# Mamba-2 scan layer: cumulative sums one convolution tile sooner, the first group's decay on VectorE behind its x tiles, its exponentials behind the last silu

## The chip, the core and the metric

The kernel runs on one core of a Trainium2 chip (trn2). The metric is the device time of one execution in microseconds (us). The engines of the core are named as the profile names them: PE is TensorE (matmuls; PEld its weight loads), DVE is VectorE, ACT is ScalarE, POOL is GpSimd, and SP only starts DMA transfers here.

## The reference, cut to what matters

Two macaron layers: each is half a SwiGLU, a mixer, half a SwiGLU, with a layer norm behind each. Layer 0 mixes with sparse attention, layer 1 with a Mamba-2 scan. The change lies in that scan, over 256 tokens in two chunks of 128, with 32 heads in 4 groups of 8:

```python
z, xbc, dt = split(x @ w_in)            # gate 2048, x/B/C 2048+512+512, dt 32
xbc = silu(conv_b + sum_k xbc_pad[:, k:k+seq] * conv_w[k])   # 4 taps
xs, b_in, c_in = split(xbc)
dt = softplus(dt + dt_bias); a_dt = dt * -exp(a_log)
a_cs = cumsum(a_dt, over the chunk)
decay = exp(where(tri, a_cs[l] - a_cs[s], -inf))             # per head, 128 x 128
y_diag = ((c @ b.T) * decay) @ (xs * dt)
states = b.T @ (xs * dt * exp(a_cs[-1] - a_cs)); prev = scan over chunks
y = y_diag + (c @ prev) * exp(a_cs) + xs * d_skip
out = rms_norm(y * silu(z), per group) * norm_g @ w_out
```

## The kernel before

All weights stream from DRAM in units of 128 x 1024 (`raw`), issued by SP. ACT casts each to a high part (`wh`, line 188), DVE subtracts to get the low part (`wl`, line 207), and PE multiplies in three passes (high by high, high by low, low by high; lines 380 to 382). Ten units fit in the ring of high and low parts. `W.pump(n)` makes the low parts that are due and then n more high parts; `W.lows()` makes only the low parts that are due and starts loads.

The order of the work is written out by hand: each engine has its instructions in the order in which the code issues them.

In `ssd` the names are these. `z_half(g, t, i, u)` is half of the gate projection of group g for chunk t, 12 matmuls, with a silu on ACT (line 1116) behind its second half. `bc_tile(i)` (8 of them) and `xs_tile(g, i, u)` (4 for each group) are convolution tiles: 24 matmuls into a PSUM bank `pxs`, one of three that take turns; then `conv`: an identity with bias on ACT (line 1135), three multiply-adds on DVE (line 1138) and a silu on ACT (line 1130). That silu is put in a list and issued only behind the identity of the next tile, or by `flush()`.

`cumsums()` multiplies `adt` by triangles on PE, takes two small exponentials on ACT (`dend`, `eacs`), copies on DVE, and has POOL store the sums to DRAM (`scr`). `decay_load(t, g)` has POOL load them back, spread over all partitions, into `M[t, g]` (128 x 1024, 8 heads). `decay_seg` subtracts the sums, head by head, 8 instructions: on ACT as a relu with the sign turned (line 1183) where `on_act` is set, else on DVE (line 1185). `decay_exp` is one exponential on ACT (line 1188), `decay_cb` a product with `cbm` (c by b, under the triangle) on DVE (line 1192).

`x_tok(t, g)` transposes the four x tiles of a group on PE (line 1207) and scales them on DVE (lines 1209, 1210). `diag(t, g)` multiplies `M[t, g]` by them (PE, line 1220), `state` and `carry` take care of the step from chunk 0 to chunk 1, `gate` adds and multiplies by the silu of z (DVE, lines 1237, 1238), `square`, `root` and `norm` scale, and `y_tr` transposes back.

Group 0's decay is made ahead of the loop over groups, between its own four x tiles, and with relus on ACT. Groups 1 to 3 make theirs inside the loop, on DVE, one group ahead. The last half of z of group 1 (`z_half(1, 1, 1, uz)`) is kept for the end of this stretch.

Of the kernel before, what the change touches and what calls it, by code (L numbers as in the profile page):

```python
# [258 lines left out]
def trunk_kernel(ctx: ExitStack, tc: tile.TileContext, widths, x, ln_g, ln_b, wts, kvg, convp,  # L259
# [12 lines left out]
    def nm(s):  # L272
        cnt[0] += 1
        return f"{s}_{cnt[0]}"
# [4 lines left out]
    def f2(s):  # L279
        return wk.tile([128, 512], F32, name=nm(s), tag="f2", bufs=9)  # L280
# [13 lines left out]
    def pmm():  # L294
        return psum.tile([128, 512], F32, name=nm("pmm"), tag="pmm", bufs=2)
# [11 lines left out]
    def ptr():  # L307
        return psum.tile([128, 512], F32, name=nm("ptr"), tag="ptr", bufs=2)

    W = Weights(nc, f4, ring, wts, widths, SLOTS, RAWS)  # L310
# [705 lines left out]
    def ssd(xT, u, ln_i):  # L1016
# [39 lines left out]
        def cumsums():  # L1056
            pt = ptr()
            for t in range(2):
                v = adt[:, t * 32:(t + 1) * 32]
                nc.tensor.matmul(pt[:, t * 32:(t + 1) * 32], tri, v, start=True, stop=True)  # L1060
                nc.tensor.matmul(pt[:32, 128 + t * 128:256 + t * 128], v, tri, start=True, stop=True)
            nc.tensor.matmul(pt[:, 64:96], after, adt[:, :32], start=True, stop=True)
            nc.scalar.activation(dend, pt[:, 64:96], AF.Exp)
            nc.scalar.activation(eacs, pt[:, 32:64], AF.Exp)
            at = f1("at")
            nc.vector.tensor_copy(at[:32], pt[:32, 128:384])
            nc.gpsimd.dma_start(scr.rearrange("t h l -> h t l"), at[:32].rearrange("p (t l) -> p t l", t=2))
            for t in range(2):
                acs[t] = tiny("acs")
                nc.vector.tensor_copy(acs[t], pt[:, t * 32:(t + 1) * 32])  # L1070
# [49 lines left out]
        def decay_load(t, g):  # L1120
            M[t, g] = f4("M")
            nc.gpsimd.dma_start(M[t, g], scr[t:t + 1, g * 8:(g + 1) * 8, :].rearrange("o h l -> o (h l)")
                                .to_broadcast([128, 1024]))
# [4 lines left out]
        def flush():  # L1128
            while late:
                nc.scalar.activation(*late.pop(0), AF.Silu)  # L1130
# [11 lines left out]
        def bc_tile(i):  # L1142
            ps = xbank()
            proj_b(ps[:, :256], xT, u + 10 + i, False)
            W.free(u + 10 + i)
            dst = bT if i < 4 else cTt
            conv(ps, 16 + i, dst[:, (i % 4) * 256:(i % 4 + 1) * 256])
            W.pump(1 + i % 2)
# [4 lines left out]
        def b_tr():  # L1153
            pt = pspare(4)
            for g in range(SG):
                nc.tensor.transpose(pt[:, g * 128:(g + 1) * 128], bT[:, g * 256:g * 256 + 128], ident)
            nc.scalar.copy(btok, pt)

        def cb(t):
            pt = pspare(4)  # L1160
            for g in range(SG):
                c = slice(g * 256 + t * 128, g * 256 + (t + 1) * 128)
                nc.tensor.matmul(pt[:, g * 128:(g + 1) * 128], bT[:, c], cTt[:, c], start=True, stop=True)
            nc.vector.tensor_mul(cbm[:, t * 512:(t + 1) * 512].rearrange("p (g l) -> p g l", g=SG),
                                 pt.rearrange("p (g l) -> p g l", g=SG),
                                 tri[:, None, :].to_broadcast([128, SG, 128]))
# [3 lines left out]
        def hv(ap):  # L1170
            return ap.rearrange("p (h d) -> p h d", h=8)

        def hb(ap, g):
            return ap[:, g * 8:(g + 1) * 8][:, :, None].to_broadcast([128, 8, 64])

        def decay_seg(t, g, on_act=False):

            m = M[t, g]
            for h in range(8):
                hs = slice(h * 128, (h + 1) * 128)  # L1180
                a = acs[t][:, g * 8 + h:g * 8 + h + 1]
                if on_act:
                    nc.scalar.activation(m[:, hs], m[:, hs], AF.Relu, bias=a, scale=-1.0)
                else:
                    nc.vector.tensor_scalar(m[:, hs], m[:, hs], a, 0.0, op0=ALU.subtract, op1=ALU.min)

        def decay_exp(t, g, on_act=False):
            nc.scalar.activation(M[t, g], M[t, g], AF.Exp, scale=-1.0 if on_act else 1.0)

        def decay_cb(t, g):  # L1190
            mv = M[t, g].rearrange("p (h l) -> p h l", h=8)
            nc.vector.tensor_mul(mv, mv, cbm[:, None, t * 512 + g * 128:t * 512 + (g + 1) * 128]
                                 .to_broadcast([128, 8, 128]))
# [4 lines left out]
        def x_tok(t, g):  # L1198

            if t:  # L1200
                pt = ptr()
            elif g < 3:
                pt = psum.tile([128, 512], F32, name=nm("pxt"), tag="acc11", bufs=1)
            else:
                pt = pmm()
            for i in range(4):
                nc.tensor.transpose(pt[:, i * 128:(i + 1) * 128], xsT[g][i][:, t * 128:(t + 1) * 128], ident)
            y[t], xd[t] = f2("xdt"), f2("xtok")
            nc.vector.tensor_mul(hv(y[t]), hv(pt), hb(dt[:, t * 32:(t + 1) * 32], g))
            nc.vector.tensor_mul(hv(xd[t]), hv(pt), hb(dsk, g))  # L1210

        def x_end(g):
            xe[g] = f2("xe")
            nc.vector.tensor_mul(hv(xe[g]), hv(y[0]), hb(dend, g))
# [43 lines left out]
        def xs_tile(g, i, uu):  # L1258
            if not i:
                xsT[g] = []  # L1260
            ps = xbank() if g < 3 else pmm()
            proj_b(ps[:, :256], xT, uu, False)
            W.free(uu)
            o = wk.tile([128, 256], F32, name=nm("xsT"), tag="xsT", bufs=5)
            conv(ps, g * 4 + i, o)
            xsT[g].append(o)
            W.pump(1)
# [29 lines left out]
        uz = u + 6  # L1297
        for i in range(8):
            bc_tile(i)
            if i == 6:  # L1300
                cumsums()
                for t in range(2):
                    decay_load(t, 0)
        u += 18
        for i in range(4):
            xs_tile(0, i, u + i)
            if i == 0:
                b_tr()
                cb(0)
                cb(1)  # L1310
                decay_seg(0, 0, True)
            elif i == 1:
                decay_seg(1, 0, True)
            elif i == 2:
                decay_exp(0, 0, True)
                decay_exp(1, 0, True)
            else:
                decay_cb(0, 0)
        z_half(1, 1, 1, uz)
        flush()  # L1320
        W.pump(2)
        decay_cb(1, 0)
        u += 4
        py = {}
        for g in range(SG):
            if g < 2:
                f = [lambda i=i: xs_tile(g + 1, i, u + i) for i in range(4)]
                f += [lambda t=t, i=i: (z_half(g + 2, t, i, u + 4), W.pump(1)) for t in range(2) for i in range(2)]
            elif g == 2:
                x3 = [lambda i=i: xs_tile(3, i, u + 2 * i) for i in range(4)]  # L1330
                o0 = [lambda i=i: out_piece(i, u + 2 * i + 1) for i in range(4)]
                f = [x3[0], x3[1], o0[0], x3[2], o0[1], x3[3], o0[2], o0[3]]
            else:
                f = [lambda i=i: out_piece(4 + i, u + i) for i in range(6)]
            f[0]()
            x_tok(0, g)
            x_tok(1, g)
            x_end(g)
            f[1]()
            f[2]()  # L1340
            py[0] = diag(0, g)
            state(g)
            gate(0, g, py[0])
            if g < 3:
                decay_load(0, g + 1)
            f[3]()
            carry(g)
            square(0)
            root(0)
            py[1] = diag(1, g)  # L1350
            gate(1, g, py[1])
            if g < 3:
                decay_load(1, g + 1)
            f[4]()
            square(1)
            root(1)
            norm(0)
            if g < 3:
                decay_seg(0, g + 1)
            f[5]()  # L1360
            y_tr(0, g)
            norm(1)
            if g < 3:
                decay_seg(1, g + 1)
                f[6]()
                flush()
                y_tr(1, g)
                decay_exp(0, g + 1)
                decay_exp(1, g + 1)
                f[7]()  # L1370
                decay_cb(0, g + 1)
                decay_cb(1, g + 1)
                W.lows()
                u += 8
# [56 lines left out]
```

## Time and profile before

| | us |
|---|---|
| median of 3 runs | 1066.45 (1066.4 to 1067.17) |
| the profiled execution | 1065.23 |
| its span, first to last instruction | 1063.4 |
| PE busy in the span | 1044.4 |
| DVE busy | 748.9 |
| ACT busy | 574.7 |

The span is 1.8 us shorter than the time of its own execution, and that execution is 1.2 us under the median. All times of instructions below are counted from the start of the span. The mean granted clock of PE is 0.993 of full speed.

### The profile page before, as it was taken

What the parts mean: (1) busy time and instruction counts of PE and PEld (TensorE: products, weight loads), DVE (VectorE), ACT (ScalarE), POOL (GpSimd) and SP (SyncE); (2) the same over time, 40 slices, a digit from 0 to 9 for tenths busy, and PEclk for the clock granted to TensorE, in tenths of its full rate; (3) what the DMA queues carried; (4) which work ended last, traced back from release to release, by engine and by line L of the source; (5) the groups of instructions that cost most, each with busy time, mean ns of one, the idle gap of its engine ahead of it and who ended that gap; (6) DMA issues with size and microseconds to landing.
All of it is one profiled execution on the core that took longest, in us unless ns stands there. A gap on an engine that the chain in (4) does not pass through costs nothing.

```text
span 1063.4 us, 15407 instructions
## 1 busy us (share of the span) xinstructions
PE 1044.4 (98%) x5859; PEld 901.1 (85%) x5859; DVE 748.9 (70%) x1191; ACT 574.7 (54%) x949; POOL 58.4 (5%) x110
## 2 busy tenths in 40 slices
PE   8999999999999999999999999997999999999997
PEld 7888888888788888888888888997889888888886
DVE  6666665799777666656766665796999976666655
ACT  6555554476636555533655553587566645555540
POOL 2000000100000000000000000140111010000001
PEclk9999999999999999999999999998999999999999
DMA  9966655252647666543766644354545665666501
GB/s 331 366 197 200 202 184 178 80 163 77 214 162 260 209 205 206 190 159 119 270 204 207 210 145 159 137 164 158 178 141 187 219 245 169 228 208 208 178 1 40
DMA packets 54729, 195.56 MB, mean 184 GB/s; under 512 B 6176, under 2 KB 6240, under 8 KB 54656
## 3 DMA queue, kind: packets, MB, share of 16 engines
q1 hardware_dynamic: 51552, 183.95, 50.7%
q0 software_dynamic: 3104, 10.64, 3.2%
q8 instruction: 46, 0.75, 0.3%
q14 instruction: 27, 0.22, 0.1%
HBM read 193.48 MB, written 1.08 MB: 183 GB/s over the span
## 4 chain that ended last, share of the span: by engine, by line
PE 88%; DVE 4%; issue 2%; ACT 2%; POOL 2%; DMA 1%; SPq 0%; POOLq 0%; DVEq 0%; ACTq 0%
PE ptr L480 12%; PE pmm L480 12%; PE acc L380 9%; PE acc L381 9%; PE acc L382 9%; PE ptr L482 6%; PE pmm L482 6%; PE pmm L382 4%; PE pmm L380 4%; PE pmm L381 4%; DVE wl L207 2%; PE psp L380 1%; PE psp L381 1%; PE psp L382 1%; PE ptr L1220 1%
## 5 line engine op out<-in xcount | busy, mean ns | idle before, releaser
L207 DVE TENSOR_TENSOR wl<-raw,wh 128x1024 fp32r<-128x1024 f32 (+2 forms) x334 | 394.5, 1211 | 154.8 <-ACT wh L188 153.9
L188 ACT CAST wh<-raw 128x1024 fp32r<-128x1024 f32 (+2 forms) x334 | 335.1, 1036 | 44.5 <-PE acc L382 38.9
L480 PE MATMUL pmm<-xT,wh 128*128 128x512 f32 x576 | 144.0, 392 | 0.0
L480 PE MATMUL ptr<-xT,wh 128*128 128x512 f32 x576 | 143.5, 391 | 0.4 <-DVE hL L377 0.4
L380 PE MATMUL acc<-wh,hH 128*128 128x512 f32 (+1 forms) x352 | 137.4, 390 | 0.0
L381 PE MATMUL acc<-wl,hH 128*128 128x512 f32 (+1 forms) x352 | 137.1, 389 | 0.0
L382 PE MATMUL acc<-wh,hL 128*128 128x512 f32 (+1 forms) x352 | 136.3, 387 | 0.0
L480 PEld LDWEIGHTS ptr<-xT,wh 128*128 128x128 f32 x576 | 105.6, 188 | 20.9 <-DVE hL L377 0.6
L480 PEld LDWEIGHTS pmm<-xT,wh 128*128 128x128 f32 x576 | 105.3, 188 | 20.1
L642 ACT CAST hH<-h 128x256 fp32r<-128x256 f32 x72 | 29.3, 406 | 112.2 <-DVE h L638 112.2
L482 PEld LDWEIGHTS pmm<-xT,wl 128*128 128x128 f32 x576 | 78.6, 190 | 5.6
L482 PEld LDWEIGHTS ptr<-xT,wl 128*128 128x128 f32 x576 | 78.6, 190 | 5.6
L482 PE MATMUL ptr<-xT,wl 128*128 128x256 f32 x576 | 80.3, 282 | 0.0
L482 PE MATMUL pmm<-xT,wl 128*128 128x256 f32 x576 | 80.3, 282 | 0.0
L382 PEld LDWEIGHTS acc<-wh,hL 128*128 128x128 f32 x352 | 66.1, 188 | 14.1
L380 PEld LDWEIGHTS acc<-wh,hH 128*128 128x128 f32 x352 | 66.4, 189 | 11.8
L381 PEld LDWEIGHTS acc<-wl,hH 128*128 128x128 f32 x352 | 66.4, 189 | 11.1
L631 ACT ACTIVATE sil<-gate 128x256 f32<-128x256 f32 x72 | 30.1, 419 | 79.2 <-DVE gate L489 79.2
L380 PE MATMUL pmm<-wh,xT 128*128 128x512 f32 (+2 forms) x184 | 71.8, 390 | 0.0
L382 PE MATMUL pmm<-wh,xT 128*128 128x512 f32 (+2 forms) x184 | 70.7, 384 | 0.2 <-DVE xT L377 0.2
L381 PE MATMUL pmm<-wl,xT 128*128 128x512 f32 (+2 forms) x184 | 70.0, 380 | 0.0
L643 DVE TENSOR_TENSOR hL<-h,hH 128x256 fp32r<-128x256 f32 x72 | 30.6, 425 | 34.0 <-ACT hH L642 34.0
(277 smaller groups left out, 1573.5 us busy)
## 6 DMA issues: line engine op xcount, KB each, us to landing
raw<-in_wts_dram SPq DMA_DIRECT2D x339, 512.0 KB, 4.2
M<-scr POOLq DMA_DIRECT2D x8, 512.0 KB, 5.1
lng<-in_ln_g_dram POOLq DMA_DIRECT2D x6, 512.0 KB, 4.3
lnb<-in_ln_b_dram POOLq DMA_DIRECT2D x6, 512.0 KB, 4.8
raw<-in_wts_dram SPq DMA_DIRECT2D x4, 408.0 KB, 3.7
x<-in_x_dram SPq DMA_DIRECT2D x4, 256.0 KB, 5.9
out_dram<-x SPq DMA_DIRECT2D x4, 256.0 KB, 2.1
raw<-in_wts_dram SPq DMA_DIRECT2D x2, 492.0 KB, 4.1
```

The lines of the kernel that those rows point to most:

```text
L188: nc.scalar.copy(h[:, c:c + n], raw[:, c:c + n])
L207: self.nc.vector.tensor_sub(lo[:, s], raw[:, s], h[:, s].bitcast(F32))
L380: nc.tensor.matmul(ps, lh, rh, start=first, stop=False)
L381: nc.tensor.matmul(ps, lh, rl, start=False, stop=False)
L382: nc.tensor.matmul(ps, ll, rh, start=False, stop=last)
L480: nc.tensor.matmul(ps, H[:, k * 128:(k + 1) * 128], xT.HL[:, k, :], start=k == 0, stop=False)
L482: nc.tensor.matmul(ps[:, :SEQ], L[:, k * 128:(k + 1) * 128], xT.H[:, k, :], start=False, stop=k == DK - 1)
L631: nc.scalar.activation(sil, gate, AF.Silu)
L642: nc.scalar.copy(hH[j // 2][:, s], h)
L643: nc.vector.tensor_sub(hL[j // 2][:, s], h, hH[j // 2][:, s].bitcast(F32))
L1220: nc.tensor.matmul(py[:, h * 64:(h + 1) * 64], m[:, h * 128:(h + 1) * 128], y[t][:, h * 64:(h + 1) * 64], start=True, stop=True)
```

## The change

The cumulative sums, their store and group 0's two loads are issued behind convolution tile 5 of b and c instead of tile 6. Between the four x tiles of group 0 only the transposes of b and the products of c and b remain. The subtraction for chunk 0 (`decay_seg(0, 0)`) is issued on DVE behind the fourth x tile; then come the last half of z, the last silu, both `x_tok` of group 0, the subtraction for chunk 1 on DVE, and both exponentials. `W.pump(2)` at that place becomes `W.lows()`. In the loop, group 0 has its two `decay_cb` where the other groups have `x_tok`.

```diff
@@ -1297,7 +1297,7 @@
         for i in range(8):
             bc_tile(i)
-            if i == 6:
+            if i == 5:
                 cumsums()
                 for t in range(2):
                     decay_load(t, 0)
@@ -1308,18 +1308,15 @@
                 b_tr()
                 cb(0)
                 cb(1)
-                decay_seg(0, 0, True)
-            elif i == 1:
-                decay_seg(1, 0, True)
-            elif i == 2:
-                decay_exp(0, 0, True)
-                decay_exp(1, 0, True)
-            else:
-                decay_cb(0, 0)
+        decay_seg(0, 0)
         z_half(1, 1, 1, uz)
         flush()
-        W.pump(2)
-        decay_cb(1, 0)
+        x_tok(0, 0)
+        x_tok(1, 0)
+        decay_seg(1, 0)
+        decay_exp(0, 0)
+        decay_exp(1, 0)
+        W.lows()
         u += 4
         py = {}
         for g in range(SG):
@@ -1333,8 +1330,12 @@
             f[0]()
-            x_tok(0, g)
-            x_tok(1, g)
+            if g:
+                x_tok(0, g)
+                x_tok(1, g)
+            else:
+                decay_cb(0, 0)
+                decay_cb(1, 0)
             x_end(g)
             f[1]()
             f[2]()
```

What this does to the order on three engines, at the end of group 0's x tiles. In the rows a name's number tells one buffer from another.

PE before, around the transposes of group 0 (line 1207); the rows above them belong to the first x tile of group 1:

```order
L381 MATMUL pxs_7456<-xT_6625,wh_7110 128x256
L382 MATMUL pxs_7456<-xT_6625,wl_7111 128x256
L1207 MATMUL pxt_7496<-ident,xsT_7268 128x128
L1207 MATMUL pxt_7496<-ident,xsT_7332 128x128
L1207 MATMUL pxt_7496<-ident,xsT_7378 128x128
L1207 MATMUL pxt_7496<-ident,xsT_7418 128x128
L1207 MATMUL ptr_7505<-ident,xsT_7268 128x128
```

PE now, at the same transposes; the rows above them are the end of the last half of z, and the row below begins the first x tile of group 1:

```order
L381 MATMUL ptr_6892<-wl_6692,xT_6625 128x512
L382 MATMUL ptr_6892<-wh_6691,xT_6625 128x512
L1207 MATMUL pxt_7435<-ident,xsT_7268 128x128
L1207 MATMUL pxt_7435<-ident,xsT_7324 128x128
L1207 MATMUL pxt_7435<-ident,xsT_7362 128x128
L1207 MATMUL pxt_7435<-ident,xsT_7400 128x128
L1207 MATMUL ptr_7444<-ident,xsT_7268 128x128
L1207 MATMUL ptr_7444<-ident,xsT_7324 128x128
L1207 MATMUL ptr_7444<-ident,xsT_7362 128x128
L1207 MATMUL ptr_7444<-ident,xsT_7400 128x128
L380 MATMUL pxs_7466<-xT_6625,wh_7110 128x256
```

The eight transposes have moved ahead of the 24 matmuls of that x tile.

ACT before, from the subtraction for chunk 1 to the silu of the fourth x tile (`xsT_7418`):

```order
L1183 ACTIVATE M_7204<-M_7204,acs_7200 128x128 x8
L1135 ACTIVATE cv_7379<-pxs_7353,convp_sb 128x256
L1130 ACTIVATE xsT_7332<-cv_7333 128x256
L188 CAST wh_7388<-raw_7238 128x1024
L1188 ACT_TABLE_LOAD
L1188 ACTIVATE M_7202<-M_7202 128x1024
L1188 ACTIVATE M_7204<-M_7204 128x1024
L1135 ACTIVATE cv_7419<-pxs_7393,convp_sb 128x256
L1130 ACT_TABLE_LOAD
L1130 ACTIVATE xsT_7378<-cv_7379 128x256
L188 CAST wh_7428<-raw_7276 128x1024
L1116 ACTIVATE zs_6789<-ptr_6892 128x512
```

ACT now, from the identity of the fourth x tile (`cv_7401`) to the first silu of group 1:

```order
L1135 ACTIVATE cv_7401<-pxs_7375,convp_sb 128x256
L1130 ACTIVATE xsT_7362<-cv_7363 128x256
L188 CAST wh_7410<-raw_7276 128x1024
L1116 ACTIVATE zs_6789<-ptr_6892 128x512
L1130 ACTIVATE xsT_7400<-cv_7401 128x256
L1188 ACT_TABLE_LOAD
L1188 ACTIVATE M_7165<-M_7165 128x1024
L1188 ACTIVATE M_7167<-M_7167 128x1024
L1135 ACTIVATE cv_7492<-pxs_7466,convp_sb 128x256
L188 CAST wh_7497<-raw_7332 128x1024
L1135 ACTIVATE cv_7530<-pxs_7504,convp_sb 128x256
L1130 ACT_TABLE_LOAD
```

The 16 relus are gone from ACT, and the two exponentials stand behind the silu of the fourth x tile, ahead of the identity of group 1's first x tile (`cv_7492`).

DVE before, from the fourth x tile's multiply-adds (`cv_7419`) to those of group 1's first tile (`cv_7482`) and the scalings of `x_tok`:

```order
L1138 SCALAR_TENSOR_TENSOR cv_7419<-pxs_7393,convp_sb,cv_7419 128x253
L207 TENSOR_TENSOR wl_7389<-raw_7238,wh_7388 128x1024
L1192 TENSOR_TENSOR M_7202<-M_7202,cbm_6686 128x1024
L207 TENSOR_TENSOR wl_7429<-raw_7276,wh_7428 128x1024
L1192 TENSOR_TENSOR M_7204<-M_7204,cbm_6686 128x1024
L1138 SCALAR_TENSOR_TENSOR cv_7482<-pxs_7456,convp_sb,cv_7482 128x255
L1138 SCALAR_TENSOR_TENSOR cv_7482<-pxs_7456,convp_sb,cv_7482 128x254
L1138 SCALAR_TENSOR_TENSOR cv_7482<-pxs_7456,convp_sb,cv_7482 128x253
L207 TENSOR_TENSOR wl_7450<-raw_7340,wh_7449 128x1024
L207 TENSOR_TENSOR wl_7453<-raw_7386,wh_7452 128x1024
L1209 TENSOR_TENSOR xdt_7501<-pxt_7496,dt_6674 128x512
L1210 TENSOR_TENSOR xtok_7502<-pxt_7496,dsk 128x512
```

DVE now, from the fourth x tile's low part to the first product with `cbm`:

```order
L207 TENSOR_TENSOR wl_7373<-raw_7238,wh_7372 128x1024
L1185 TENSOR_SCALAR M_7165<-M_7165,acs_7161 128x128 x8
L1209 TENSOR_TENSOR xdt_7440<-pxt_7435,dt_6674 128x512
L1210 TENSOR_TENSOR xtok_7441<-pxt_7435,dsk 128x512
L1209 TENSOR_TENSOR xdt_7449<-ptr_7444,dt_6674 128x512
L1210 TENSOR_TENSOR xtok_7450<-ptr_7444,dsk 128x512
L1185 TENSOR_SCALAR M_7167<-M_7167,acs_7163 128x128 x8
L207 TENSOR_TENSOR wl_7411<-raw_7276,wh_7410 128x1024
L1138 SCALAR_TENSOR_TENSOR cv_7492<-pxs_7466,convp_sb,cv_7492 128x255
L1138 SCALAR_TENSOR_TENSOR cv_7492<-pxs_7466,convp_sb,cv_7492 128x254
L1138 SCALAR_TENSOR_TENSOR cv_7492<-pxs_7466,convp_sb,cv_7492 128x253
L1192 TENSOR_TENSOR M_7165<-M_7165,cbm_6686 128x1024
```

The 16 subtractions are new on DVE, `x_tok` and they stand ahead of group 1's first tile, and two low parts (`wl`) that stood ahead of `x_tok` come later, one behind each following tile.

## Rows read from the trace of the kernel before

**Rows 1.** The first part of the page: busy time of each engine, its share of the span, and its instructions.

```profile
PE 1044.4 (98%) x5859; PEld 901.1 (85%) x5859; DVE 748.9 (70%) x1191; ACT 574.7 (54%) x949; POOL 58.4 (5%) x110
```

**Rows 2.** Who PE waited for in the scan layer, 680 to 850 us: us in total, times, the longest in us.

```profile
PE pxt L1207 <- ACT xsT L1130: 5.9, 2, 4.6
PE ptr L1220 <- DVE xdt L1237: 0.4, 1, 0.4
PE pmm L1163 <- ACT cTt L1130: 0.4, 1, 0.4
```

**Rows 3.** PE in order of time: start us, us, what, count, and in brackets the idle time before it and what ended it. The cumulative sums, the start of the last half of z, group 1's x tiles, the transposes of group 0, the chunk products (line 1220) with the carry between them, the transposes behind the norm (line 1254) and, from 773 us, the transposes of group 1.

```profile
710.72 0.30 PE L1060 MATMUL ptr<-adt,tri 128*128 128x32 f32 x2
...
729.52 0.40 PE L380 MATMUL ptr<-wh,xT 128*128 128x512 f32 x1
...
732.27 0.28 PE L380 MATMUL pxs<-xT,wh 128*128 128x256 f32 x1
...
735.14 0.38 PE L1207 MATMUL pxt<-ident,xsT 128*128 128x128 f32 x2
740.16 0.48 PE L1207 MATMUL pxt<-ident,xsT 128*128 128x128 f32 x1 [4.64 <-ACT xsT L1130]
741.90 0.48 PE L1207 MATMUL pxt<-ident,xsT 128*128 128x128 f32 x1 [1.26 <-ACT xsT L1130]
...
742.88 0.56 PE L380 MATMUL pxs<-xT,wh 128*128 128x256 f32 x1
...
749.96 1.90 PE L1220 MATMUL ptr<-xdt,M 128*128 128x64 f32 x16
...
755.47 1.02 PE L1232 MATMUL ptr<-st,cTt 128*128 128x512 f32 x2
756.93 2.00 PE L1220 MATMUL ptr<-xdt,M 128*128 128x64 f32 x16 [0.43 <-DVE xdt L1237]
...
764.43 0.66 PE L1254 MATMUL ptr<-ident,xdt 128*128 128x128 f32 x4
...
773.74 0.60 PE L1207 MATMUL pxt<-ident,xsT 128*128 128x128 f32 x4
...
774.53 0.36 PE L380 MATMUL pxs<-xT,wh 128*128 128x256 f32 x1
```

**Rows 4.** Stretches of one us around that stop: length, busy time of each engine with its instructions, the granted clock of PE, the DMA share and GB/s.

```profile
738.00:739.00 1.00, 0.00 (x0) 0.00 (x0) 0.55 (x2) 0.98 (x2) 0.00 (x0) 0.95 0.71 283
739.00:740.00 1.00, 0.00 (x0) 0.00 (x0) 0.96 (x3) 0.99 (x2) 0.00 (x0) 0.50 0.01 4
...
746.00:747.00 1.00, 1.00 (x11) 1.00 (x10) 1.00 (x2) 0.00 (x0) 0.00 (x0) 1.00 0.06 25
```

**Rows 5.** ACT in order of time, columns as in Rows 3: the first table load and small exponential behind the cumulative sums, the relus for chunk 0, the two exponentials, an identity, the silu of z ahead of the last silu; then, in group 0, the square of chunk 1 and the norm of chunk 0.

```profile
714.15 1.28 ACT L1063 ACT_TABLE_LOAD   x1
715.45 0.20 ACT L1063 ACTIVATE dend<-ptr 128x32 f32<-128x32 f32 x1
...
726.41 2.45 ACT L1183 ACTIVATE M<-M,acs 128x128 f32<-128x128 f32 x8 [5.37 <-DMA M<-scr]
...
735.92 2.00 ACT L1188 ACTIVATE M<-M 128x1024 f32<-128x1024 f32 x2
737.83 0.55 ACT L1135 ACTIVATE cv<-pxs,convp_sb 128x256 f32<-128x256 f32 x1
...
740.95 0.59 ACT L1116 ACTIVATE zs<-ptr 128x512 f32<-128x512 f32 x1
...
763.04 0.63 ACT L1242 ACTIVATE xtok<-xdt 128x512 f32<-128x512 f32 x1 [4.68 <-DVE xdt L1238]
...
763.67 0.71 ACT L1249 ACTIVATE xdt<-xdt,rs 128x512 f32<-128x512 f32 x1
```

**Rows 6.** DVE in order of time, columns as in Rows 3: a low part ahead of the copies of the sums, multiply-adds of x tiles, a product with cbm, low parts, the first scaling of x_tok, the first gate, the subtractions for chunk 1 of group 1.

```profile
712.61 1.22 DVE L207 TENSOR_TENSOR wl<-raw,wh 128x1024 fp32r<-128x1024 f32 x1
...
729.35 1.52 DVE L1138 SCALAR_TENSOR_TENSOR cv<-pxs,convp_sb,cv 128x255 f32<-128x255 f32 x3 [6.13 <-ACT cv L1135]
...
740.98 1.22 DVE L1192 TENSOR_TENSOR M<-M,cbm 128x1024 f32<-128x1024 f32 x1
...
744.38 1.51 DVE L1138 SCALAR_TENSOR_TENSOR cv<-pxs,convp_sb,cv 128x255 f32<-128x255 f32 x3
745.81 2.35 DVE L207 TENSOR_TENSOR wl<-raw,wh 128x1024 fp32r<-128x1024 f32 x2
748.08 0.68 DVE L1209 TENSOR_TENSOR xdt<-pxt,dt 128x512 f32<-128x512 f32 x1
748.68 0.68 DVE L1210 TENSOR_TENSOR xtok<-pxt,dsk 128x512 f32<-128x512 f32 x1
...
756.19 0.68 DVE L1237 TENSOR_TENSOR xdt<-ptr,xtok 128x512 f32<-128x512 f32 x1
...
767.51 1.66 DVE L1185 TENSOR_SCALAR M<-M,acs 128x128 f32<-128x128 f32 x8 [1.07 <-DMA M<-scr]
```

**Rows 7.** POOL in order of time, columns as in Rows 3: the store of the sums and the issue of group 0's two loads; then, from the view of the tile M, how long its eight loads took from issue to landing.

```profile
717.01 0.69 POOL L1067 DMA_DIRECT2D scr<-at  x1 [11.66 <-DVE acs L1070]
720.75 1.10 POOL L1122 DMA_DIRECT2D M<-scr  x2 [3.06 <-ACT wh L188]
...
DMA to landing us min/median/max: 4.3/5.1/7.8
```

## Prediction

> **What bounds the kernel now.** I read the page's busy times first, then who PE waited for, then PE, ACT and DVE in order of time around the place found. PE is busy for 98% of the span [rows 1], so only what keeps PE from running, or makes it run slowly, is worth anything. In the whole scan layer PE waits for another engine four times, 6.7 us in all [rows 2]; 5.9 of it lies at one place, the transposes of group 0's x tiles.
>
> Seen from PE [rows 3]: the last half of z runs from 729.52 to 732.27, group 1's first x tile to 735.14; two transposes run; the third waits 4.64 us and the fourth 1.26 us, for silus on ACT. During that stop the granted clock falls from full (2.4 GHz) to half (1.2 GHz): 0.95 in the stretch from 738, after PE had stood still since about 735.5, then 0.50; it is full again in the stretch from 746 [rows 4]. So the work behind the stop is slow too: group 1's second and third x tiles take 742.88 to 749.96, 7.08 us, where one at full clock takes 735.14 - 732.27 = 2.87, so 1.34 us are lost there.
>
> Seen from ACT [rows 5]: its queue stands 5.37 us for the load of M and then does 2.45 us of relus, while identities of finished x tiles stand behind them. DVE starves with it: 6.13 us idle ahead of the second tile's multiply-adds [rows 6]. The x tiles' silus are late because decay work holds ACT's queue.
>
> **Part by part.** I walk the changed order with the durations of this trace until the diagonal product of chunk 1 (before: 756.93 [rows 3]), because from there on all engines have the same order as before but for two weight units.
>
> *Sums one tile sooner.* PE reaches them one tile earlier, at 710.72 - 2.87 = 707.8 [rows 3]. POOL's last work for them ended at 717.01 - 11.66 = 705.35 [rows 7], so PE doesn't wait. On DVE the copies follow the low part at 712.61 [rows 6], so the store leaves near 714.4 instead of 717.01 and the loads near 718.2 instead of 720.75 [rows 7]. They land by 718.2 + 0.5 + 7.8 = 726.5 at the latest [rows 7], and are first read at 732.5. That is free; it hides behind four tiles.
>
> ACT's two small exponentials and two table loads move one tile forward too. ACT then has the last silu of c ready at 719.0, where PE wants it at 719.3: the 0.4 us wait of [rows 2] goes.
>
> *Relus off ACT.* 16 relus, 2 x 2.45 = 4.9 us of ACT, and its wait of 5.37 for the load leave the queue [rows 5]. The identities then start when PE ends each tile, and the first three silus are ready before PE gets to the transposes.
>
> *Transposes ahead of the x tile.* PE ends z's last half at 732.27 - 0.4 = 731.9 and goes straight to the transposes. The fourth needs the fourth silu, which stands behind z's own silu: before, PE resumed 741.90 - 740.95 = 0.95 after that silu began [rows 3, 5]. Now z's silu begins at about 732.05, the fourth transpose at 733.0. Three transposes take 3 x 0.11 ((774.53 - 773.74) / 8 is 0.10, [rows 3]), so PE waits 0.8 us. The rest and three x tiles follow: 0.5 + 2.9 + 2.87 + 2.87, to 742.1.
>
> *Subtractions on DVE, exponentials behind the last silu.* DVE gets the fourth tile's identity at 729.9 (the tile ends near 729.3, the identity takes 0.55 [rows 5]). From there it has no gap: multiply-adds 1.43, low part 1.13 (745.81 - 744.38; half of 748.08 - 745.81), eight subtractions 1.6, four scalings at 0.60, eight subtractions 1.6 [rows 6]: 729.9 to 738.1. ACT waits for these with the second exponential, begins it at 738.15, and, 0.96 later ((737.83 - 735.92) / 2 [rows 5]), starts the identity of group 1's first tile, finished at 739.7. This is the wait that the change adds. Behind it stand that identity, then the next ones and their silus, and DVE waits 0.5 for it.
>
> DVE goes on: multiply-adds to 741.15, products with cbm to 742.3 and 743.4 (1.13 apart), scaling 744.0, multiply-adds 745.45, low part 746.6, multiply-adds 748.0, low part 749.15, gate to 749.85.
>
> PE: the diagonal product of chunk 0 needs the first of those products (its end: 742.4), 0.35 us after PE is free. Then product, state and x tile take 755.47 - 749.96 = 5.51, to 747.95; the carry 756.93 - 0.43 - 755.47 = 1.03, to 749.0. The product of chunk 1 needs the gate and starts at 749.9, after 0.9 us.
>
> *Two units fewer made ahead.* `W.pump(2)` is gone, so two casts (about 1.0 each) and two low parts (1.13 each) move into group 0's stage. They cost nothing: the units are used a group later. The casts fit in ACT's idle 4.68 us ahead of the second square [rows 5], the low parts partly in DVE's idle 1.07 us ahead of group 1's subtractions [rows 6] and in later gaps. If that cover is gone, they cost up to 2 x 1.13 = 2.3. Two weight loads on SP now wait for buffers that the product and the gate of chunk 1 free; their casts come over 12 us after that, and loads land in 4.3 to 7.8 us [rows 7].
>
> **The sum.** Against the profiled execution (1065.23, of which 1063.4 is the span): 749.9 instead of 756.93 is 7.0 us, to 1058.2. Of it 9.0 us are PE's removed losses (731.9 + 0.8 + 2.95 + 2 x 2.87 + 5.51 + 1.03 = 747.9 would be PE's time without any wait), and 0.8 + 0.35 + 0.9 = 2.05 are new waits. The median stood 1.22 above that execution, so 1066.45 - 7.0 = **1059.4**.
>
> Waits of this kind aren't in the trace at these places, so I bound them: none at all (9.0 gained, 1057.5), or all three plus the uncovered low parts (7.0 - 2.3 = 4.7, 1061.8). I keep the walked value, since every duration in it is from a row of the same instruction. That PE's clock stays full I take from [rows 4]: it was still full in part of the stretch from 738, with PE standing since about 735.5, and these stops are under 1 us.
>
> **A page on table loads.** In [rows 5] a table load takes 1.28 us, and the exponential begins 0.02 us after its end (714.15 + 1.28 = 715.43, then 715.45); so a switch is counted here at 1.28. The Trainium skill (ScalarE: Activation LUTs, What ACT_TABLE_LOAD costs) says that every switch to another set costs a drain of about 1.38 us besides; by that page, an estimate, the gain would be 5.9 and the time 1060.5. The trace disagrees with it.
>
> **Rivals.**
> - *As walked*, 1058.3 to 1060.6: 0.70.
> - *DVE's debt comes due*: the norm of chunk 0 ended at 763.67 + 0.71 = 764.38, and PE's transposes began at 764.43 [rows 3, 5], so there is no slack behind the gate. If the deferred low parts push anything ahead of it, the gain is 4.7, the time 1061.8. Against: the order puts them behind both gates. 0.12.
> - *Dearer table loads*: were the two loads behind the earlier sums each as long again (1.28), ACT would have c's last silu 1.0 us after PE wants it: 6.0 gained, 1060.4. Against: the 0.02 us of above. 0.02.
> - *No new waits*: ACT and DVE run slightly ahead of the walk, 1057.5. Against: it needs 2 us on DVE, which has no gap. 0.09.
> - *It doesn't do what it says*: the fourth silu, and not the relus, held PE, and the stop moves with the transposes to the end of z; the time stays at 1066. Against: the third silu was the longer wait [rows 3], and ACT's order now has all four ahead of the exponentials. 0.04.
> - *Slower*: ACT's queue is held by the second exponential, which now needs the load for chunk 1 and the subtractions. Each us that this load lands after 736.5 (the fourth scaling's end on DVE) delays identity, product and PE by a us. At 743.5 all gain is gone, at 746 the time is 1069. Against: it should land by 726.5. 0.03.
>
> **Numbers.** A measurement of this kernel can tell about 0.2% (2.1 us) from no change. Faster by over that: 0.70 + 0.02 + 0.12 + 0.09 = 0.93; within: 0.04; slower: 0.03. The range holds all the faster cases, with a little room for the run: 1057.3 to 1062.2.
>
> **What would show it.** Right: no idle on ACT before relus, since there are none; PE's transposes of group 0 right behind z, with one stop under 1 us on the last silu; granted clock 1.00 through the stage; short PE waits at line 1220 on DVE's line 1192 and line 1237; DVE without gaps from the fourth tile to the gate. Wrong: a stop on PE above 2 us or a half clock there; waits on PE at line 1254; waits on `wl`. The prediction falls if DVE needs longer for the subtractions than 0.2 us each, or if ACT doesn't get the last silu done within 1 us of z.

## The result and the profile after

The changed kernel takes 1059.95 us (median of 6 runs, 1058.99 to 1060.45) against 1066.36 before (6 runs): a ratio of 0.994, 95% interval 0.993 to 0.995. Forecast were 1059.4 and a range of 1057.3 to 1062.2. Its profiled execution, the slowest of the six, took 1060.45, of which 1058.6 is the span.

Who PE waited for in the scan layer, 680 to 850 us, in the changed kernel (us in total, times, the longest); it answers to [rows 2]:

```profile
PE ptr L1220 <- DVE xdt L1237: 0.8, 1, 0.8
PE pxt L1207 <- ACT xsT L1130: 0.7, 1, 0.7
```

The 5.9 us at group 0's transposes have become 0.7, the wait on c's last silu is gone, and at line 1220 0.4 has become 0.8. To see the whole stretch, take a start that the change doesn't touch, the transposes of b behind group 0's first x tile. PE in order of time, before and then after (start us, us, what, count, in brackets the idle time before it and what ended it):

```profile
718.04 0.60 PE L1156 MATMUL psp<-ident,bT 128*128 128x128 f32 x4
```

```profile
720.41 0.60 PE L1156 MATMUL psp<-ident,bT 128*128 128x128 f32 x4
734.14 0.49 PE L1207 MATMUL pxt<-ident,xsT 128*128 128x128 f32 x3
735.29 0.33 PE L1207 MATMUL pxt<-ident,xsT 128*128 128x128 f32 x1 [0.66 <-ACT xsT L1130]
...
744.79 1.97 PE L1220 MATMUL ptr<-xdt,M 128*128 128x64 f32 x16
...
752.16 2.00 PE L1220 MATMUL ptr<-xdt,M 128*128 128x64 f32 x16 [0.75 <-DVE xdt L1237]
```

From the transposes of b to the diagonal product of chunk 1 it took 756.93 - 718.04 = 38.89 us before [rows 3] and takes 752.16 - 720.41 = 31.75 now: 7.14 less. From there to the end of the span it is the same: 1063.4 - 756.93 = 306.47, and 1058.6 - 752.16 = 306.44. The spans differ by only 4.8, because this execution reached the transposes of b 2.37 us later than that of before. The change has no part in that: from the first matmul of the first b tile (690.57 before, 692.94 now) to these transposes it is 27.47 us in both, so the 2.37 us arose ahead of everything that was changed. So the stretches are compared below, beside the medians.

VectorE shows where the 7.14 come from. Windows from the transposes of b to the start of VectorE's first gate (line 1237), before and then after; the columns are length, busy time of PE, PEld, DVE, ACT and POOL with their instructions, the granted clock, the DMA share and GB/s:

```profile
718.04:756.19 38.15, 31.89 (x230) 29.68 (x228) 27.75 (x41) 26.38 (x49) 1.62 (x3) 0.91 0.49 166
```

```profile
720.41:751.42 31.01, 30.22 (x230) 27.92 (x228) 28.76 (x55) 19.64 (x31) 1.61 (x3) 1.00 0.57 177
```

VectorE has 1.01 us more work (16 subtractions more, two low parts fewer), but stands 31.01 - 28.76 = 2.25 us instead of 38.15 - 27.75 = 10.40. 8.15 less idle and 1.01 more work are 7.14 us. The long waits for ACT's identities, 6.13 us the first of them [rows 6], are gone; the longest that is left is 0.83. VectorE and ACT after, in order of time; what [rows 5] had at 726.41, relus behind a wait of 5.37, isn't there any more:

```profile
732.20 1.52 DVE L1138 SCALAR_TENSOR_TENSOR cv<-pxs,convp_sb,cv 128x255 f32<-128x255 f32 x3 [0.23 <-ACT cv L1135]
...
734.80 1.65 DVE L1185 TENSOR_SCALAR M<-M,acs 128x128 f32<-128x128 f32 x8
...
742.00 1.52 DVE L1138 SCALAR_TENSOR_TENSOR cv<-pxs,convp_sb,cv 128x255 f32<-128x255 f32 x3 [0.45 <-ACT cv L1135]
743.43 2.35 DVE L1192 TENSOR_TENSOR M<-M,cbm 128x1024 f32<-128x1024 f32 x2
...
747.73 1.22 DVE L207 TENSOR_TENSOR wl<-raw,wh 128x1024 fp32r<-128x1024 f32 x1
...
750.29 1.22 DVE L207 TENSOR_TENSOR wl<-raw,wh 128x1024 fp32r<-128x1024 f32 x1
751.42 0.68 DVE L1237 TENSOR_TENSOR xdt<-ptr,xtok 128x512 f32<-128x512 f32 x1
```

```profile
734.83 0.41 ACT L1130 ACTIVATE xsT<-cv 128x256 f32<-128x256 f32 x1
735.26 1.28 ACT L1188 ACT_TABLE_LOAD   x1
736.55 1.06 ACT L1188 ACTIVATE M<-M 128x1024 f32<-128x1024 f32 x1
740.45 1.06 ACT L1188 ACTIVATE M<-M 128x1024 f32<-128x1024 f32 x1 [2.84 <-DVE M L1185]
741.42 0.55 ACT L1135 ACTIVATE cv<-pxs,convp_sb 128x256 f32<-128x256 f32 x1
```

POOL sends the sums 720.41 - 716.83 = 3.58 us ahead of the transposes of b, where it was 718.04 - 717.01 = 1.03 [rows 7]:

```profile
716.83 0.69 POOL L1067 DMA_DIRECT2D scr<-at  x1 [9.11 <-DMA raw<-in_wts_dram]
720.50 1.08 POOL L1122 DMA_DIRECT2D M<-scr  x2 [2.98 <-DMA scr<-at]
```

### The profile page after: what moved, and what is told of

Its sections match the earlier page's. It is cut to its first block, busy times and chain, and to the rows that moved or that the text cites. A ratio compares the mean times of both kernels' runs of the same rounds, so it can differ in the third digit from the quotient of the medians.

```text
span 1058.6 us, 15407 instructions
## 1 busy us (share of the span) xinstructions
PE 1044.0 (99%) x5859; PEld 900.4 (85%) x5859; DVE 752.1 (71%) x1207; ACT 569.6 (54%) x933; POOL 58.4 (6%) x110
## 4 chain that ended last, share of the span: by engine, by line
PE 91%; DVE 5%; DMA 2%; issue 1%; ACT 0%; POOL 0%; SPq 0%; POOLq 0%; DVEq 0%
PE ptr L480 12%; PE pmm L480 12%; PE acc L380 9%; PE acc L381 9%; PE acc L382 9%; PE ptr L482 6%; PE pmm L482 6%; PE pmm L382 4%; PE pmm L380 4%; PE pmm L381 4%; DVE wl L207 2%; PE pxs L380 1%; PE pxs L382 1%; PE pxs L381 1%; PE ptr L1220 1%; DMA raw<-in_wts_dram 1%
```

## The experiments

All in one table. "Stretch" runs from the transposes of b to the diagonal product of chunk 1, "rest" from there to the end of the span, both of the profiled execution and worked out as above. Ratios are to the kernel before, run beside each.

| kernel | median us | ratio, 95% interval | transposes of b at | stretch | rest |
|---|---|---|---|---|---|
| before | 1066.36 | | 718.04 | 38.89 | 306.47 |
| changed | 1059.95 | 0.994, 0.993 to 0.995 | 720.41 | 31.75 | 306.44 |
| sums early only | 1064.46 | 0.9981, 0.9972 to 0.9990 | 719.52 | 37.11 | 306.17 |
| all but early sums | 1059.80 | 0.9939, 0.9927 to 0.9952 | 719.26 | 32.24 | 306.40 |
| relus on ACT, late | 1062.46 | 0.9959, 0.9945 to 0.9972 | 720.06 | 34.36 | 306.28 |
| last silu first | 1059.05 | 0.9933, 0.9921 to 0.9946 | 718.87 | 31.75 | 306.48 |
| transposes behind tile | 1058.71 | 0.9932, 0.9918 to 0.9945 | 718.53 | 31.75 | 306.42 |
| one stop filled | 1066.60 | 1.0002, 0.9993 to 1.0010 | 719.91 | 38.86 | 306.43 |
| both stops filled | 1066.25 | 1.0000, 0.9991 to 1.0009 | 719.97 | 38.95 | 306.38 |
| two units ahead | 1065.45 | 0.9995, 0.9986 to 1.0004 | 719.32 | 38.86 | 306.12 |
| engine alone | 1062.93 | 0.9970, 0.9959 to 0.9981 | 719.60 | 35.70 | 306.40 |
| low parts late | 1063.33 | 0.9969, 0.9958 to 0.9981 | 719.44 | 32.38 | 310.08 |
| product early, low parts late | 1062.11 | 0.9957, 0.9945 to 0.9970 | 719.20 | 30.78 | 310.32 |
| one low part late | 1058.07 | 0.9927, 0.9914 to 0.9939 | 719.20 | 30.83 | 306.37 |

The gain by medians and the gain by stretch and rest agree within 0.3 us in most rows; the widest are 0.8 us apart, among them the changed kernel itself (6.4 by medians, 7.2 by the trace).

**The sums.** First they alone are moved in the kernel before, then everything but them is taken from the change.

```diff
# in the kernel before
-            if i == 6:
+            if i == 5:
# in the changed kernel
-            if i == 5:
+            if i == 6:
```

> The kernel before with one thing of the change: the cumulative sums, their store and the loads of M one tile of the convolution sooner; the relus stay on ACT where they were. Theory: ACT's queue stands 5.37 us for the load of M [rows 5], so a load that lands 2.5 us sooner (the store left 2.55 us sooner in the changed kernel) lets the relus, and the silus behind them, start 2.5 us sooner: PE's stop of 4.64 us [rows 3] shrinks to about 2.1, the 0.4 us wait on cTt [rows 2] goes, and if the granted clock then stays full, up to 1.3 to 1.8 us more come back: 2.9 to 4.7 us faster than before, 1061.7 to 1063.5. Rival 1: what holds the silus is the work that ACT has in its queue (relus, exponentials, identities), not the wait for the load: less than 1 us faster. Rival 2: the early sums alone are the whole gain: 6 us or more.

> The changed kernel with the cumulative sums put back to the tile where they were. Theory: in the changed kernel nothing reads M before VectorE's first subtraction, at 734.8 us of its trace, and the loads land some 5 us ahead of that; 2.55 us later is still in time. Only the 0.4 us wait of PE on cTt [rows 2] comes back: 0 to 0.5 us slower than the changed kernel, 5.9 to 6.4 us faster than before. Rival: the subtractions on VectorE need the early load: 2 us or more slower than the changed kernel, and a wait of VectorE on M ahead of its first subtractions.

Alone they bring 1.9 us, less than the 2.9 to 4.7 expected: the relus began 2.15 us sooner (725.74 - 719.52 against 726.41 - 718.04), PE's stop shrank to 2.99 us, but the clock still fell to 0.50 (741 to 747), and PE now reached the product of chunk 1 without a wait for the gate, by its own slow road. Left out of the change they are missed by 32.24 - 31.75 = 0.49 us, PE's 0.4 us wait on cTt in it. So in the change the early sums are nearly free of effect; the load of M has time either way, as predicted.

**Engine or place.** The relus go back to ACT but stay at the new place; then VectorE makes the subtractions, at the old place.

```diff
# in the changed kernel
-        decay_seg(0, 0)
...
-        decay_seg(1, 0)
-        decay_exp(0, 0)
-        decay_exp(1, 0)
+        decay_seg(0, 0, True)
+        decay_exp(0, 0, True)
+        decay_seg(1, 0, True)
+        decay_exp(1, 0, True)
# in the kernel before (and so for decay_seg(1, 0) and both decay_exp)
-                decay_seg(0, 0, True)
+                decay_seg(0, 0)
```

> The changed kernel, but the subtractions for both chunks stay ACT's (as relus, 2.45 us for each chunk [rows 5]); each chunk's relus stand behind the last silu, with the chunk's exponential behind them. So the place is the changed kernel's and the engine is the old one. Theory: the order of ACT's queue takes away PE's long stops, and VectorE's part is only that ACT is free for the identity of group 1's first tile (start 741.42 us in the changed kernel's trace). With the relus ACT reaches it at 735.26 + 1.28 + 2 x (2.45 + 0.96) = 743.4, 2.0 us later, and VectorE's chain to the gate hangs on it: 1.5 to 2.2 us slower than the changed kernel, 4 to 5 us faster than before, no stop of PE above 3 us. Rival 1: the place alone matters: within 0.3 us of the changed kernel. Rival 2: the engine is everything: within 1.5 us of the kernel before.

> The kernel before with VectorE making the subtractions in place of ACT's relus, everything at the old places: sums, subtractions, exponentials, transposes. Theory: the change's gain has two halves that overlap. With ACT free of the load's wait and of 4.9 us of relus [rows 5] the third silu no longer holds PE 4.64 us, but the two exponentials with their two table loads still stand ahead of the last two silus, and VectorE now stands for the load of M: a stop of 0.5 to 2 us stays, and the gate comes 4 to 5 us sooner: 4 to 5 us faster than before. Rival 1: the place is the whole gain: less than 1.5 us faster than before. Rival 2: the engine is the whole gain: 6 us or more faster.

With the relus on ACT it is 2.5 us slower than the changed kernel by medians, 2.61 in the stretch, a little more than the 1.5 to 2.2 expected: the products with cbm start 1.87 us later (744.95 - 720.06 against 743.43 - 720.41), and the 1.98 us stop of PE that this makes is followed by a clock of 0.50 (748 to 750), which costs the other 0.74. With the engine alone the gain is 3.2, less than the 4 to 5 expected. VectorE's window up to its first gate:

```profile
719.60:754.56 34.96, 31.75 (x230) 29.37 (x228) 30.81 (x57) 22.21 (x34) 1.63 (x3) 0.95 0.56 185
```

PE's stops are only 1.42 and 1.41 us there. What holds the gate is VectorE: it stands 34.96 - 30.81 = 4.15 us instead of 10.40, 3.65 of it ahead of its first subtraction for the load of M, and has 3.06 us more work than before, since the subtractions come in and the low parts of the two units stay.

**PE's stops.** The last silu is put ahead of the half of z, so that the 0.66 us stop goes; or the transposes are put back behind the x tile, which covers the silu as well.

```diff
# last silu first
-        z_half(1, 1, 1, uz)
         flush()
+        z_half(1, 1, 1, uz)
# transposes behind tile
-        x_tok(0, 0)
-        x_tok(1, 0)
...
-            if g:
-                x_tok(0, g)
-                x_tok(1, g)
-            else:
+            x_tok(0, g)
+            x_tok(1, g)
+            if not g:
```

> The changed kernel with the identity and silu of the fourth x tile issued ahead of the last half of z (the changed kernel has them behind it), so that the silu for which the fourth transpose waits 0.66 us no longer stands behind z's own silu on ACT. Theory: the end of this stretch is set by VectorE's chain to the gate of chunk 0, not by PE; the 0.66 us stop goes and comes back as a longer wait at line 1220: within 0.25 us of the changed kernel. Rival: PE's stops add up, so each is worth its length: 0.66 us faster than the changed kernel.

> The changed kernel with the transposes of group 0, and the scalings behind them, put back behind group 1's first x tile. Theory: VectorE's chain to the gate has the same work in it in another order; the 0.66 us stop of PE goes because the tile covers the last silu, and comes back at line 1220; within 0.5 us of the changed kernel either way. So the place of the transposes is no part of the gain. Rival: it is a part of it: 1 us or more slower than the changed kernel.

Both have the stretch of the changed kernel to the hundredth, 31.75. The stop has moved, as PE of the kernel with the last silu first shows:

```profile
743.26 1.97 PE L1220 MATMUL ptr<-xdt,M 128*128 128x64 f32 x16 [0.99 <-DVE M L1192]
```

The medians are 0.9 and 1.2 us lower, with intervals that overlap that of the changed kernel; the traces show no work or wait for it but the start of the transposes of b, which lies upstream. So where PE stops is of no weight here, nor where the transposes stand; VectorE's chain to the gate decides.

**The half clock.** PE gets work for its stops in the kernel before: 36 matmuls ahead of the third transpose in a first run, then 11 more ahead of the fourth in a second, whose edit is shown.

```diff
             for i in range(4):
+                if not t and not g and i > 1:
+                    if i == 2:
+                        idle = pmm()
+                    for _ in range(36 if i == 2 else 11):
+                        nc.tensor.matmul(idle[:, :256], xT.H[:, 0, :128], xT.H[:, 0, :], start=True, stop=True)
```

> The kernel before, with 36 matmuls of 128x256 put between the second and the third transpose of group 0, where PE stands 4.64 us for the silu [rows 3]; their result is not used. They only fill the stop. Theory: PE lost more there than its waits, because the granted clock fell to half during the stop and the two x tiles behind it ran slowly [rows 3, 4]. Kept at work, PE waits as long for the silus, but the clock stays at 1.00 and the 1.34 us of the two tiles and some 0.4 us of the transposes come back: 1.2 to 1.8 us faster than before. Rival: the clock has no part in it, since VectorE's chain to the gate sets the time (PE waits 0.43 us for the gate there): 0 to 0.4 us faster, and PE's wait for the gate grows instead.

> The kernel before with both stops of PE at group 0's transposes filled: 36 matmuls of 128x256 ahead of the third transpose, 11 ahead of the fourth; their result is not used. With the first stop alone filled, the granted clock still fell to half, later and for about 3 us. Theory: VectorE's chain to the gate sets the time there, and PE's slow clock costs next to nothing, since PE waits for the gate anyway: within 0.5 us of before, with the clock at 1.00 and PE's wait for the gate grown from 0.43 to about 1.5 us. Rival: the slow clock was a cost of its own, and its 1.34 us come back: 1.2 to 1.8 us faster than before.

The first didn't settle it: nothing is gained, but the clock fell none the less, to 0.50 in the two windows from 745, behind the 1.41 us stop that was left. In the second it stays at 1.00 in every window from 734 to 760, and nothing is gained either. PE there, with the lines moved by 5, and VectorE's window up to its first gate:

```profile
750.80 2.00 PE L1225 MATMUL ptr<-xdt,M 128*128 128x64 f32 x16 [0.41 <-DVE xdt L1214]
...
753.29 1.10 PE L1231 MATMUL ptr<-xe,btok 128*128 128x512 f32 x2 [0.48 <-DVE xe L1219]
...
758.92 2.00 PE L1225 MATMUL ptr<-xdt,M 128*128 128x64 f32 x16 [0.81 <-DVE xdt L1242]
```

```profile
719.97:758.18 38.21, 36.42 (x277) 33.72 (x275) 27.79 (x42) 26.80 (x50) 1.63 (x3) 1.00 0.52 174
```

VectorE reaches its gate as late as before, 38.21 us behind the transposes of b against 38.15. The 1.34 us that the two slow tiles had cost come back as waits for VectorE, 0.41 + 0.48 + 0.81 = 1.70 against 0.43 before; at the gate alone 1.5 were expected. So the first theory of the clock falls: before the change the half clock lay beside VectorE's chain and cost nothing.

**The two units.** The changed kernel makes them ahead again.

```diff
         decay_exp(1, 0)
-        W.lows()
+        W.pump(2)
```

> The changed kernel with the two weight units made ahead as before the change (two casts on ACT, and their low parts on VectorE, ahead of group 1's first tile) in place of only finishing the open low part. Theory: VectorE's chain from the fourth tile to the gate has no room, so two more low parts of 1.13 us in it [rows 6], less the 0.45 us that VectorE waits there in the changed kernel's trace, and two casts of 1.0 us ahead of the identity on ACT, make the gate 1.8 to 2.3 us later: 1.5 to 2.3 us slower than the changed kernel. So part of the change's gain is that these units moved behind the gates, which cost nothing there. Rival: the units cost nothing at either place: within 0.4 us of the changed kernel.

This takes back 7.1 us in the stretch and 5.5 by medians: nearly the whole gain, and far more than the 1.5 to 2.3 expected. ACT, VectorE and PE of this kernel, and its windows of one us:

```profile
740.33 1.98 ACT L188 CAST wh<-raw 128x1024 fp32r<-128x1024 f32 x2
742.21 0.56 ACT L1135 ACTIVATE cv<-pxs,convp_sb 128x256 f32<-128x256 f32 x1
```

```profile
742.80 1.52 DVE L1138 SCALAR_TENSOR_TENSOR cv<-pxs,convp_sb,cv 128x255 f32<-128x255 f32 x3 [2.34 <-ACT cv L1135]
744.23 2.35 DVE L207 TENSOR_TENSOR wl<-raw,wh 128x1024 fp32r<-128x1024 f32 x2
746.50 2.35 DVE L1192 TENSOR_TENSOR M<-M,cbm 128x1024 f32<-128x1024 f32 x2
...
754.49 0.68 DVE L1237 TENSOR_TENSOR xdt<-ptr,xtok 128x512 f32<-128x512 f32 x1
```

```profile
747.87 3.65 PE L1220 MATMUL ptr<-xdt,M 128*128 128x64 f32 x16 [4.28 <-DVE M L1192]
...
758.18 1.89 PE L1220 MATMUL ptr<-xdt,M 128*128 128x64 f32 x16
```

```profile
745.00:746.00 1.00, 0.00 (x0) 0.00 (x0) 1.00 (x2) 0.99 (x2) 0.00 (x0) 0.95 0.00 0
746.00:747.00 1.00, 0.00 (x0) 0.00 (x0) 1.00 (x2) 1.00 (x3) 0.00 (x0) 0.50 0.49 102
...
755.00:756.00 1.00, 1.00 (x7) 1.00 (x6) 0.87 (x2) 0.00 (x0) 0.00 (x0) 0.50 0.96 393
```

The casts hold the identity 1.88 us, the low parts the products 2.27 more: they start at 746.50 - 719.32 = 27.18 behind the transposes of b, not at 23.02. PE stands 4.28 us for them, its clock falls to half, and this time VectorE doesn't cover it: from the product of chunk 0 to that of chunk 1 it is 758.18 - 747.87 = 10.31 us instead of 7.37. 1.88 + 2.27 + 2.94 are the 7.1.

VectorE's gate starts 754.49 - 719.32 = 35.17 us behind the transposes of b, 4.16 later than in the changed kernel but still 2.98 sooner than before. PE arrives last here, on its half clock; that its stretch (38.86) is that of before (38.89) is chance. So it doesn't follow that the units alone are the gain. They were not taken out of the kernel before by themselves. PE waited there only 0.43 us for the gate and not at all for the product of chunk 0 [rows 2, 3], so an estimate from these rows is some 0.4 us. The parts of the change don't add up, because each shortens the chain only until another engine is last.

**Low parts later still.** With the last silu first, four low parts that stand in group 0's stage are made behind the gate of chunk 1; then the product of chunk 0 is put ahead of chunk 1's subtractions besides; then, in the changed kernel, one low part alone is put off.

```diff
# low parts late (make_only is set in group 0's stage): x tiles of group 1 only make the high parts, the pieces of z behind the gates the low parts
-            W.pump(1)
+            if make_only:
+                W.highs(1)
+            else:
+                W.pump(1)
...
+                    elif t + i:
+                        W.lows(len(W.late) - 2)
+                        W.highs(1)
# product early, besides
+        decay_exp(0, 0)
         x_tok(0, 0)
         x_tok(1, 0)
+        decay_cb(0, 0)
         decay_seg(1, 0)
-        decay_exp(0, 0)
...
-                decay_cb(0, 0)
# one low part late (late is 1 in the third x tile of group 1, 2 in the fourth): the one makes the high part alone, the other keeps one low part
-            W.pump(1)
+            if late > 0:
+                W.lows(late - 1 and 1 or len(W.late))
+                W.highs(1)
+            else:
+                W.pump(1)
```

> The changed kernel with the last silu ahead of the half of z, and with the low parts that VectorE makes of weights in group 0's x tiles made behind the gate of chunk 1 instead. Theory: VectorE's chain to the gate of chunk 0 has two low parts of 1.13 us in it behind the product of chunk 0; without them it is 2.27 us shorter there, and PE's wait for the gate, 0.75 us in the changed kernel's trace, goes. The wait for the product of chunk 0, 0.99 us with the last silu first, stays, since no low part stands in that part of the chain while VectorE has nothing to wait for: 0.7 to 0.9 us faster than the changed kernel. Rival: the low parts are only put off; behind the gate of chunk 1 they delay the norm, for which PE's transposes have no slack: as fast as the changed kernel or up to 2.3 us slower.

> As the kernel with the last silu first and the low parts late, and besides it the exponential and the product of chunk 0 stand ahead of chunk 1's subtractions on VectorE. Theory: now neither the product nor the gate of chunk 0 holds PE, the whole of the waits at line 1220 (0.99 + 0.75 us) goes: 1.4 to 1.75 us faster than the changed kernel, the least that PE allows. Rival: chunk 1's exponential, 1.1 us later, holds the identity of group 1's first tile on ACT, and with it the gate: no faster than the kernel beside it.

> The changed kernel with one low part of weights (1.13 us of VectorE) moved from ahead of the gate of chunk 0 to behind the gate of chunk 1; where four of them were moved, the time behind the diagonal product of chunk 1 grew by 3.7 us. Theory: one fits. PE's 0.75 us wait for the gate goes, and the later work has room for 1.13 us: 0.5 to 0.8 us faster than the changed kernel. Rival: VectorE has no room there (95% busy from 760 to 845 us in the changed kernel's trace): PE waits as much later: within 0.2 us of the changed kernel, or slower.

The first two are slower than the changed kernel, by 3.4 and 2.2 us. In the first PE doesn't wait for the gate of chunk 0 any more, as expected, but the stretch is 0.63 longer: the clock falls to half behind the product of chunk 0, and from there to that of chunk 1 it takes 751.82 - 743.82 = 8.00 us instead of 7.37. With the product early the stretch is 0.97 shorter, less than the 1.4 to 1.75 expected, since PE now waits 0.98 us for another result of VectorE (line 1214). In both the rest is 3.6 to 3.9 longer: the debt comes due. ACT and then PE of the kernel with the low parts late:

```profile
761.32 1.05 ACT L188 CAST wh<-raw 128x1024 fp32r<-128x1024 f32 x1 [1.44 <-DMA raw<-in_wts_dram]
```

```profile
763.52 0.66 PE L1254 MATMUL ptr<-ident,xdt 128*128 128x128 f32 x4 [1.07 <-ACT xdt L1249]
...
776.99 1.97 PE L1220 MATMUL ptr<-xdt,M 128*128 128x64 f32 x16 [0.56 <-DVE xdt L1209]
779.38 1.10 PE L1226 MATMUL ptr<-xe,btok 128*128 128x512 f32 x2 [0.42 <-DVE xe L1214]
...
785.07 2.00 PE L1220 MATMUL ptr<-xdt,M 128*128 128x64 f32 x16 [0.86 <-DVE xdt L1237]
```

A cast waits 1.44 us for a load of weights, with a norm behind it in ACT's queue; then PE waits four times, 2.91 us, where the changed kernel has no wait. A late low part keeps its raw buffer, so loads that start late fit these rows; that link was not tried by itself. One low part late is the gain that was expected and a little more: the stretch is 0.92 shorter (0.5 to 0.8 expected), the rest unchanged, and PE's only wait in the layer is this one:

```profile
PE pxt L1207 <- ACT xsT L1130: 0.7, 1, 0.7
```

By its median, 1058.07, it beats both kernels; its interval still overlaps that of the changed kernel at 0.993 to 0.9939, so that the 0.9 us rest on the trace.

## Why the prediction was right

- **The walk.** Forecast was a product of chunk 1 that starts 7.0 us sooner; it was 7.14, of which the medians show 6.4. The table agrees at the other end: the rest is 306.1 to 306.5 in all kernels but the two with a debt.
- **The waits added.** Forecast 0.8 for the fourth silu, 0.35 for the product of chunk 0, 0.9 for the gate; measured 0.66, none, 0.75. The second exponential begins at 740.45 and the identity 0.97 later (0.96 walked); VectorE waits 0.45 us for it (0.5 forecast).
- **The sums.** They hide, as said; without them 0.49 is lost, 0.4 of which was forecast.
- **The split of the gain** is the step that didn't hold. "9.0 us are PE's removed losses" was half a us too much even for PE: the stretch without its two waits is 31.75 - 0.66 - 0.75 = 30.34 us, 8.55 less than before, so that PE's own work was walked 0.45 too short and its waits 0.64 too long (2.05 against 1.41). And 1.34 of it, the slow tiles, was no loss: with the clock at full, both stops filled, the kernel before was as slow. The gain is VectorE's 8.15 us of idle time less 1.01 of work. The time came out because VectorE was walked too, and the gate taken from it.
- **Two units fewer** "cost nothing": true of where they went (306.44 against 306.47). What their going was worth had no term of its own; it stood only in VectorE's walk, which had no low parts between the multiply-adds and the products. With them there nearly everything is lost. The bound of 2.3 counted two low parts alone; ahead of group 1's first tile they cost that, their casts 1.88 more, and the half clock behind PE's stop another 2.94.
- **Rivals.** *DVE's debt* did not come in the change; it came when four low parts were put off, and cost 3.6 to 3.9 (2.3 was put on two). *Dearer table loads*: the silu ahead of the load ended at 734.83 + 0.41 = 735.24, the load began at 735.26 and ended at 736.54, and the exponential starts at 736.55. The drain that the Trainium skill adds (ScalarE: Activation LUTs, What ACT_TABLE_LOAD costs) is not in this trace either, ahead of the load or behind it. *It doesn't do what it says*, *Slower* and *No new waits* fall with the rows on PE above.

## What to carry to other kernels

Walk every engine to the point where the stretch ends, and take the gain from the one that arrives last: its idle time less its added work. A stop on another engine, even on the busiest, and even one with a half clock behind it, may be worth nothing, until the chain that covers it gets shorter. What a change drops in passing, here two units made ahead, deserves a term of its own, since moved work pays only if the queue that it is moved into is empty.

## What the runs showed of the hardware

Executions differ by some 2 us before the scan layer begins. PE reached the transposes of b between 718.04 and 720.41 us in 14 profiles, but in all of them 27.47 to 27.48 us behind the first matmul of the first b tile, and the first matmul of line 480, in layer 0, already lay between 32.6 and 34.9 us. So a single span can't tell a difference of 2 us in a later stretch, while a stretch between two events can.

The granted clock did not follow a stop alone. With the last silu first, PE stood 0.99 us ahead of line 1220 and kept 1.00; with the transposes behind the tile it stood 1.00 us there, and kept 1.00 too. With the low parts late, after the same 0.99 us at the same place, it fell to 0.57 in the window from 746 and to 0.50 in the two behind it, with PE at work. In the kernel with two units ahead it stayed at 0.50 for some 8 us behind the stop, with PE at work there too. Why the equal stops differ stays open.
